# Moving the first score products of group 0 in layer 1 further back in TensorE's stream

## The chip, the cores and the metric

One core of a Trainium2 chip runs the whole computation in one launch. The metric is device time in microseconds (us); the kernel before took 1233.0 us, the median of three runs (1233.14, 1230.1 and 1233.0).

## The reference, cut to what matters

Two layers act on x (512 positions by 1024 features, fp32). Layer 0 has a mixer of gated linear attention and differential attention, layer 1 a mixer of dilated window attention; each is followed by a gated feed-forward block with a short convolution. The change lies in layer 1's mixer:

```
z = (h @ w_in).reshape(B, S, 3 groups, 3 (q, k, v), 4 heads, 128)
q = rmsnorm(z[:, :, :, 0], q_gain);  k = rmsnorm(z[:, :, :, 1], k_gain);  v = z[:, :, :, 2]
for each group g, (window, dilation) in (128, 1), (512, 4), (2048, 16):
    s = q k^T / sqrt(128), causal, inside the window, keys at stride dilation
    o_g = softmax(s) v,  lse_g = log of the softmax denominator
o = sum over g of softmax over g (lse_g) * o_g;   x = x + o @ w_out
```

## The kernel before, in words

**Products.** Every weight product is done in three passes: weights and activations are split into a high and a low part (`hi`, `lo`; `hhi`, `hlo`), and high times high, high times low and low times high are summed in PSUM. The weights come as a chain of slabs; `load_next` (L168 on) loads a slab through SP's queue, ScalarE makes `hi` (L179), VectorE makes `lo` (L182). There are three buffers for each, and a slab is asked for when the slab two places ahead of it is begun.

**Layer 1's mixer.** Its order is q, k of group 0, q, k of group 1, q, k of group 2, then v of the three groups. In this text they are q0, k0, q1, k1, q2, k2, v0, v1, v2. Each is a `tok_gemm` (L333): 4 slabs of 2 contraction chunks; for each slab the four position tiles t = 0 to 3 in turn, 6 products of 128x512 for a tile, so 24 a slab and 96 a projection. Each tile has a PSUM bank from a pool of eight (`bufs=8`). In the last slab a tile is complete after its 6 products and is evicted.

**Eviction of q and k** (`qk_evict`, L396 on): ScalarE squares the bank (L367), VectorE sums (L369), both work out the reciprocal root (L213 to L218), VectorE scales the bank into `qn` (L401, the last reader of the bank), VectorE turns 32x32 blocks (L387), ScalarE's queue writes them to DRAM (`turned`, L389), POOL's queue reads them back in four DMAs into `z` (L394; three `z` buffers), and ScalarE copies `z` into q (L416) or k (L414).

**Scores** (`scores`, L893 on). Group 0 has four steps, one for a query tile; each writes two banks (L901), 8 products of 128x128 in the first step and of 128x256 in the other three. All four k tiles of group 0 are needed for its first step, because its positions are stored by residue. Groups 1 and 2 use one bank a step (L912) and need only tile t of q and k. Behind each step VectorE masks and takes the row minimum (L282), ScalarE exponentiates (L891). After group 0's last step `residues` issues five small DMAs on POOL's queue (L930, L932), read much later in `factors`.

**What sets the order.** TensorE's order is written out by hand: `now` is a planned clock. Every step of a projection adds its planned time (`pe`), then `fire` runs each event that is due. In `tok_gemm` a step is one tile of one slab: 6 products, 3 * 2 * 512 * 0.216 / 512 = 1.296 us of planned time. An event is put down with `at(delay, ...)`. The copy of tile t into q or k is due 11.5 + t after its eviction; behind the copy of k's last tile `after_k` puts down the first score step; each score step adds its own planned time (0.86 or 1.73 us in group 0) and puts down the next 5.0 later. The orders of the other engines are worked out from the program when it is built.

Of the kernel before, what the change touches and what calls it, by code (L numbers as in the profile page):

```python
# [129 lines left out]
def trunk_kernel(ctx: ExitStack, tc: tile.TileContext, x, weights, params, lqks, w_a2, consts, out):  # L130
# [12 lines left out]
    def bank():  # L143
        return ps.tile([P, 512], F32, name="bank")
# [147 lines left out]
    def at(delay, fn, tag):  # L292
        count[0] += 1
        heapq.heappush(events, (now[0] + delay, count[0], tag, fn))
# [5 lines left out]
    def pe(us):  # L300
        now[0] += us
# [132 lines left out]
    with tc.tile_pool(name="m0", bufs=1) as m0, tc.tile_pool(name="t0", bufs=2) as t0:  # L434
        def t8(name, dt=F32):
            return m0.tile([P, 4, 512], dt, name=name, tag="t8", bufs=8)
# [143 lines left out]
        def after_k(t):  # L580
            if t == NT - 1:
                at(1.0, lambda: diff_scores(0), "diff")
# [288 lines left out]
    with tc.tile_pool(name="m1", bufs=1) as m1:  # L871
# [13 lines left out]
        def probs(dst, sc, g, t, h):  # L885

            nk = sc.shape[1]
            m = masks[:, 3 - nk // P:3].rearrange("p a b -> p (a b)") if g == 0 else masks[:, 3 * (g - 1)]
            nm = st[g][:, t, 0, h:h + 1]
            masked(dst, sc, m, nm)  # L890
            A.activation(dst, dst, AF.Exp, bias=nm, scale=-1.0, accum_out=st[g][:, t, 1, h:h + 1])  # L891

        def scores(g, t, q, k):  # L893
            ts = slice(t * P, (t + 1) * P)
            if g == 0:
                nk = P if t == 0 else 2 * P
                for hp in range(2):
                    sc = bank()
                    for h in range(2):
                        o = h * 256  # L900
                        T.matmul(sc[:, o:o + nk], q[:, 2 * hp + h, ts], k[:, 2 * hp + h, (t + 1) * P - nk:(t + 1) * P],  # L901
                                 start=(h == 0), stop=(h == 1))
                    pe(8 * nk * PASS)
                    for h in range(2):
                        b0 = max(0, 2 * t - 1)
                        dst = PR[0][:, 2 * hp + h, b0:b0 + nk // P].rearrange("p b k -> p (b k)")
                        probs(dst, sc[:, h * 256:h * 256 + nk], 0, t, 2 * hp + h)
            else:
                sc = bank()
                for h in range(4):  # L910
                    hs = slice(h * P, (h + 1) * P)
                    T.matmul(sc[:, hs], q[:, h, ts], k[:, h, ts], start=(h == 0), stop=(h == 3))  # L912
                pe(0.87)
                for h in range(4):
                    probs(PR[g][:, h, t], sc[:, h * P:(h + 1) * P], g, t, h)
            if t < NT - 1:
                at(5.0, lambda: scores(g, t + 1, q, k), "scores")
            elif g == 0:
                residues()
            elif g == 2:  # L920
                factors()
# [6 lines left out]
        def residues():  # L928

            G.dma_start(d0, st0.rearrange("p t a h -> p t (a h)"))  # L930
            for t in range(NT):
                G.dma_start(s0[32 * t:32 * t + 32].rearrange("p r a h -> p r (a h)"),  # L932
                            d0.rearrange("(r l) t c -> t l r c", r=4)[t])

        def factors():

            sn = [s0, st[1], st[2]]
            mx = m1.tile([P, NT, 4], F32, name="mx")
            V.tensor_tensor(out=mx, in0=sn[0][:, :, 0], in1=sn[1][:, :, 0], op=ALU.min)
            V.tensor_tensor(out=mx, in0=mx, in1=sn[2][:, :, 0], op=ALU.min)  # L940
            eg = m1.tile([P, 3, NT, 4], F32, name="eg")
            for g in range(3):
                V.tensor_tensor(out=eg[:, g], in0=mx, in1=sn[g][:, :, 0], op=ALU.subtract)
            A.activation(eg.rearrange("p g t h -> p (g t h)"), eg.rearrange("p g t h -> p (g t h)"), AF.Exp)
            den = m1.tile([P, NT, 4], F32, name="den")
            dt = m1.tile([P, NT, 4], F32, name="dt")
            V.tensor_tensor(out=den, in0=eg[:, 0], in1=sn[0][:, :, 1], op=ALU.mult)
            for g in (1, 2):
                V.tensor_tensor(out=dt, in0=eg[:, g], in1=sn[g][:, :, 1], op=ALU.mult)
                V.tensor_tensor(out=den, in0=den, in1=dt, op=ALU.add)  # L950
            V.reciprocal(den, den)
            for g in range(3):
                V.tensor_tensor(out=eg[:, g], in0=eg[:, g], in1=den, op=ALU.mult)

            G.dma_start(e0, eg[:, 0])
            for r in range(4):
                G.dma_start(f0[32 * r:32 * r + 32], e0.rearrange("(t l) r h -> r l t h", t=NT)[r])
            fac.extend((f0, eg[:, 1], eg[:, 2]))
            for i in range(12):
                at(10.0 + 3.5 * i, lambda i=i: weigh(i // 4, i % 4), "weigh")  # L960
# [32 lines left out]
        def after_k(g, q, k):  # L993
            def f(t):
                if t == NT - 1:
                    at(2.5 if g == 0 else 1.0, lambda: scores(g, 0, q, k), "scores")
            return f

        def by_tile(dst, r):
# [9 lines left out]
        for g in range(3):  # L1009
            q, k = t8("q"), t8("k")  # L1010
# [41 lines left out]
```

## Time and profile before

| What | Value |
|---|---|
| Median of the runs | 1233.0 us (1230.1 to 1233.14, 3 runs) |
| Profiled execution, own time | 1230.4 us |
| Profiled execution, span | 1228.6 us |
| Mean granted TensorE clock | 0.997 of full speed |
| DMA over the span | mean 103 GB/s |

The profile lists one execution. PE is TensorE's products, PEld its weight loads, DVE VectorE, ACT ScalarE, POOL GpSimd. A busy time counts instructions that do work; a wait is put down to the instruction that came last. Starts are us from the start of the span, durations in us.

### The profile page before, as it was taken

What the parts mean: (1) busy time and instruction counts of PE and PEld (TensorE: products, weight loads), DVE (VectorE), ACT (ScalarE), POOL (GpSimd) and SP (SyncE); (2) the same over time, 40 slices, a digit from 0 to 9 for tenths busy, and PEclk for the clock granted to TensorE, in tenths of its full rate; (3) what the DMA queues carried; (4) which work ended last, traced back from release to release, by engine and by line L of the source; (5) the groups of instructions that cost most, each with busy time, mean ns of one, the idle gap of its engine ahead of it and who ended that gap; (6) DMA issues with size and microseconds to landing.
All of it is one profiled execution on the core that took longest, in us unless ns stands there. A gap on an engine that the chain in (4) does not pass through costs nothing.

```text
span 1228.6 us, 15071 instructions
## 1 busy us (share of the span) xinstructions
PE 1215.2 (99%) x5687; PEld 1006.4 (82%) x5687; DVE 779.3 (63%) x1474; ACT 546.6 (44%) x896; POOL 68.4 (6%) x131
## 2 busy tenths in 40 slices
PE   9999999999999999999998999999999999999998
PEld 7888788788888888888886888889888888888887
DVE  7557868787753775366756676444877537763673
ACT  6446655454422443144534655544544314431441
POOL 0000000000000000000022324300000000000000
PEclk9999999999999999999999999999999999999999
DMA  7222111323323323332455456421233232332322
GB/s 256 87 87 70 49 56 38 100 88 102 103 86 103 99 91 103 94 91 71 137 159 169 123 162 203 140 87 51 88 103 95 94 103 93 96 103 88 101 77 95
DMA packets 41160, 127.14 MB, mean 103 GB/s; under 512 B 6359, under 2 KB 7288, under 8 KB 41088
## 3 DMA queue, kind: packets, MB, share of 16 engines
q1 hardware_dynamic: 32400, 110.38, 29.1%
q0 software_dynamic: 3936, 7.41, 2.3%
q10 hardware_dynamic: 4752, 8.39, 1.8%
q8 instruction: 44, 0.72, 0.2%
q14 instruction: 28, 0.23, 0.1%
HBM read 116.70 MB, written 8.41 MB: 102 GB/s over the span
## 4 chain that ended last, share of the span: by engine, by line
PE 95%; DMA 2%; DVE 1%; POOL 1%; ACT 0%; issue 0%; SPq 0%; POOLq 0%; ACTq 0%; DVEq 0%
PE bank L766 39%; PE bank L333 22%; PE bank L808 20%; PE bank L350 7%; DMA z<-turned 1%; PE bank L989 1%; PE bank L536 1%; PE bank L570 1%; DMA turned<-turn 1%; PE bank L901 1%; PE bank L912 1%; PE bank L379 1%; POOL z L394 1%; PE bank L974 1%; PE bank L558 0%; PE bank L664 0%
## 5 line engine op out<-in xcount | busy, mean ns | idle before, releaser
L179 ACT ACTIVATE hi<-raw 128x1024 fp32r<-128x1024 f32 (+2 forms) x209 | 217.0, 1039 | 280.7 <-PE bank L808 143.2
L182 DVE TENSOR_TENSOR lo<-raw,hi 128x1024 fp32r<-128x1024 f32 (+2 forms) x209 | 250.5, 1199 | 128.8 <-ACT hi L179 120.1
L766 PE MATMUL bank<-hhi,hi 128*128 128x512 f32 x704 | 273.9, 389 | 0.0
L766 PE MATMUL bank<-hhi,lo 128*128 128x512 f32 x704 | 273.9, 389 | 0.0
L766 PE MATMUL bank<-hlo,hi 128*128 128x512 f32 x704 | 273.9, 389 | 0.0
L333 PE MATMUL bank<-hi,hhi 128*128 128x512 f32 (+2 forms) x480 | 185.2, 386 | 0.5 <-ACT hi L179 0.5
L333 PE MATMUL bank<-lo,hhi 128*128 128x512 f32 (+2 forms) x480 | 181.1, 377 | 0.2 <-DVE lo L182 0.2
L333 PE MATMUL bank<-hi,hlo 128*128 128x512 f32 (+2 forms) x480 | 180.5, 376 | 0.0
L766 PEld LDWEIGHTS bank<-hhi,hi 128*128 128x128 f32 x704 | 132.2, 188 | 27.5
L766 PEld LDWEIGHTS bank<-hhi,lo 128*128 128x128 f32 x704 | 132.2, 188 | 27.4
L766 PEld LDWEIGHTS bank<-hlo,hi 128*128 128x128 f32 x704 | 132.2, 188 | 27.3
L808 PE MATMUL bank<-ghi,lo 128*128 128x512 f32 (+1 forms) x358 | 138.0, 385 | 0.0
L808 PE MATMUL bank<-glo,hi 128*128 128x512 f32 (+1 forms) x358 | 138.0, 385 | 0.0
L808 PE MATMUL bank<-ghi,hi 128*128 128x512 f32 (+1 forms) x358 | 138.0, 385 | 0.0
L333 PEld LDWEIGHTS bank<-lo,hhi 128*128 128x128 f32 x480 | 90.4, 188 | 17.7 <-DVE lo L182 1.0
L333 PEld LDWEIGHTS bank<-hi,hhi 128*128 128x128 f32 x480 | 90.6, 189 | 17.1 <-ACT hi L179 1.0
L333 PEld LDWEIGHTS bank<-hi,hlo 128*128 128x128 f32 x480 | 90.7, 189 | 15.4
L813 DVE TENSOR_TENSOR xT<-xT,bank 128x512 f32<-128x512 f32 (+1 forms) x49 | 33.0, 675 | 106.4 <-PE bank L808 106.2
L394 POOL DMA_DIRECT2D z<-turned x96 | 52.0, 549 | 514.0 <-DVE rs_a L213 435.9
L808 PEld LDWEIGHTS bank<-ghi,hi 128*128 128x128 f32 x358 | 67.2, 188 | 13.6
L808 PEld LDWEIGHTS bank<-glo,hi 128*128 128x128 f32 x358 | 67.2, 188 | 13.5
L808 PEld LDWEIGHTS bank<-ghi,lo 128*128 128x128 f32 x358 | 67.3, 188 | 13.5
(203 smaller groups left out, 1358.7 us busy)
## 6 DMA issues: line engine op xcount, KB each, us to landing
raw<-in_weights_dram SPq DMA_DIRECT2D x189, 512.0 KB, 3.5
raw<-in_weights_dram SPq DMA_DIRECT2D x16, 384.0 KB, 3.1
turned<-turn ACTq DMA_DIRECT2D x24, 256.0 KB, 2.9
z<-turned POOLq DMA_DIRECT2D x96, 64.0 KB, 3.8
xT<-in_xT_dram SPq DMA_DIRECT2D x7, 256.0 KB, 5.8
out_dram<-xT ACTq DMA_DIRECT2D x7, 256.0 KB, 2.0
raw<-in_weights_dram SPq DMA_DIRECT2D x2, 544.0 KB, 3.5
vt<-vs POOLq DMA_DIRECT2D x16, 64.0 KB, 2.2
```

The lines of the kernel that those rows point to most:

```text
L179: r = A.activation(hi[:, c0:c1], raw[:, c0:c1], AF.Copy)
L182: V.tensor_tensor(out=lo[:, c0:c1], in0=raw[:, c0:c1], in1=hi.bitcast(F32)[:, c0:c1], op=ALU.subtract)
L333: T.matmul(ps[t][:, :n], lhs(a[:, kc], t), b[:, k, :n], start=(kc == 0 and j == 0), stop=(kc == DC - 1 and j == 2))
L350: T.matmul(ps, w[:, k, d * P:(d + 1) * P], r(k), start=(k == 0 and j == 0), stop=(k == nk - 1 and j == 2))
L379: T.transpose(pt[:, h * P:(h + 1) * P], src[:, h * P:(h + 1) * P], ident)
L394: G.dma_start(to[32 * j:32 * j + 32].rearrange("c i b r -> c i (b r)"), d[j])
L536: T.matmul(sc[:, :nk], qT[rs, h, n * P:(n + 1) * P], kT[rs, h, :nk], start=True, stop=True)
L570: T.matmul(po[n][:, h * P:(h + 1) * P], wT[:, j * P:(j + 1) * P], bv[:, j, h * P:(h + 1) * P], start=(h == 0 and j == 0), stop=(h == 3 and ...
L766: T.matmul(ps, w[:, kc], r[:, kc], start=(kc == 0 and m == 0), stop=(kc == DC - 1 and m == 2))
L808: T.matmul(ps[:, ts], a[:, k], b[f0 + k][:, ts], start=(k == 0 and m == 0), stop=(k == n - 1 and m == 2))
L813: V.tensor_tensor(out=xT[:, c, ts], in0=xT[:, c, ts], in1=ps[:, ts], op=ALU.add)
L901: T.matmul(sc[:, o:o + nk], q[:, 2 * hp + h, ts], k[:, 2 * hp + h, (t + 1) * P - nk:(t + 1) * P], start=(h == 0), stop=(h == 1))
```

## The change

The delay between the last k copy and the first score step of group 0 goes from 2.5 to 10.5 on the planned clock. Nothing else is edited.

```
         def after_k(g, q, k):
             def f(t):
                 if t == NT - 1:
-                    at(2.5 if g == 0 else 1.0, lambda: scores(g, 0, q, k), "scores")
+                    at(10.5 if g == 0 else 1.0, lambda: scores(g, 0, q, k), "scores")
             return f
```

## Rows read from the trace of the kernel before

**Rows 1.** The page: part 1 (busy time, share of the span, instructions of each engine) and the first line of part 4 (share of the chain that ended last, by engine).
```profile
PE 1215.2 (99%) x5687; PEld 1006.4 (82%) x5687; DVE 779.3 (63%) x1474; ACT 546.6 (44%) x896; POOL 68.4 (6%) x131
PE 95%; DMA 2%; DVE 1%; POOL 1%; ACT 0%; issue 0%; SPq 0%; POOLq 0%; ACTq 0%; DVEq 0%
```

**Rows 2.** The view of waits of the whole span: engine, tile and line, what it waited for, us in total, times, longest.
```profile
PEld bank L901 <- ACT k L414: 6.2, 1, 6.2
PE bank L901 <- ACT k L414: 5.8, 1, 5.8
...
PEld bank L570 <- issue: 2.9, 5, 0.8
```

**Rows 3.** The timeline of PE around group 0's first score step: start, duration, instruction; in brackets the idle time before it and its releaser.
```profile
649.70 0.39 PE L333 MATMUL bank<-hi,hhi 128*128 128x512 f32 x1
...
667.15 0.39 PE L333 MATMUL bank<-lo,hhi 128*128 128x512 f32 x1
673.35 2.08 PE L901 MATMUL bank<-k,q 128*128 128x128 f32 x8 [5.81 <-ACT k L414]
675.08 0.77 PE L333 MATMUL bank<-hi,hhi 128*128 128x512 f32 x1
675.65 0.63 PE L333 MATMUL bank<-hi,hlo 128*128 128x512 f32 x1
...
681.54 1.89 PE L901 MATMUL bank<-k,q 128*128 128x256 f32 x8
```

**Rows 4.** Windows: length, busy time and count of each engine, granted clock, share of the DMA engines, GB/s.
```profile
649.60:667.40 17.80, 17.80 (x80) 14.52 (x78) 10.78 (x33) 5.67 (x13) 7.26 (x14) 1.00 0.57 169
667.40:673.40 6.00, 0.19 (x2) 0.05 (x1) 5.04 (x10) 3.28 (x7) 1.42 (x3) 0.73 0.67 209
673.40:677.20 3.80, 3.80 (x14) 3.37 (x15) 1.03 (x9) 1.73 (x8) 1.17 (x3) 0.53 0.24 88
677.20:707.30 30.10, 30.10 (x135) 25.15 (x134) 18.98 (x61) 18.73 (x49) 10.23 (x19) 1.00 0.46 133
```

**Rows 5.** The chain that ended last, in order of time: start, length, what, with the number of products.
```profile
673.35 2.08 PE bank L901 x8
675.43 6.27 PE bank L333 x24
681.70 1.73 PE bank L901 x8
683.42 5.45 PE bank L333 x24
...
697.78 25.85 PE bank L333 x114
723.64 0.89 PE bank L912 x8
724.53 5.46 PE bank L333 x24
729.98 0.89 PE bank L912 x8
```

**Rows 6.** Timelines of ACT and POOL: the way of k0's last tile (k0's first copy, which frees the buffer; the four reads into z; the square of q1's tile 0; k0's last copy).
```profile
665.50 0.63 ACT L414 ACTIVATE k<-z 128x512 f32<-128x512 f32 x1 [8.25 <-DMA turned<-turn]
...
666.65 2.17 POOL L394 DMA_DIRECT2D z<-turned  x4 [0.42 <-issue]
...
668.98 0.67 ACT L367 ACTIVATE sq<-bank,rstd 128x512 f32<-128x512 f32 x1
...
672.67 0.63 ACT L414 ACTIVATE k<-z 128x512 f32<-128x512 f32 x1 [1.58 <-DMA z<-turned]
```

**Rows 7.** The timeline of DVE: the scaling of a bank into qn, after which the bank is free. In order: k0's tiles 0, 1 and 3; q1's tiles 0, 1 with 2, and 3; k1's tile 1.
```profile
651.08 0.69 DVE L401 TENSOR_TENSOR qn<-bank,rr 128x512 f32<-128x512 f32 x1
...
654.29 0.68 DVE L401 TENSOR_TENSOR qn<-bank,rr 128x512 f32<-128x512 f32 x1
...
659.60 0.68 DVE L401 TENSOR_TENSOR qn<-bank,rr 128x512 f32<-128x512 f32 x1
...
671.97 0.69 DVE L401 TENSOR_TENSOR qn<-bank,rr 128x512 f32<-128x512 f32 x1
...
684.09 1.28 DVE L401 TENSOR_TENSOR qn<-bank,rr 128x512 f32<-128x512 f32 x2
...
687.99 0.69 DVE L401 TENSOR_TENSOR qn<-bank,rr 128x512 f32<-128x512 f32 x1
...
710.96 0.68 DVE L401 TENSOR_TENSOR qn<-bank,rr 128x512 f32<-128x512 f32 x1
```

**Rows 8.** Timelines of ACT and DVE: the two parts of k1's second slab (hi on ACT, lo on DVE).
```profile
667.51 1.04 ACT L179 ACTIVATE hi<-raw 128x1024 fp32r<-128x1024 f32 x1
...
668.58 1.23 DVE L182 TENSOR_TENSOR lo<-raw,hi 128x1024 fp32r<-128x1024 f32 x1 [0.24 <-ACT hi L179]
```

**Rows 9.** Timelines of POOL and ACT: the five DMAs of `residues`, the first reads of k1's tiles, and the copy of k1's tile 0.
```profile
700.07 0.57 POOL L930 DMA_DIRECT2D d<-st  x1 [4.92 <-ACT PR L891]
702.07 2.17 POOL L932 DMA_DIRECT2D s<-d  x4 [1.44 <-DMA d<-st]
711.90 2.17 POOL L394 DMA_DIRECT2D z<-turned  x4 [7.66 <-DMA turned<-turn]
...
716.44 0.63 ACT L414 ACTIVATE k<-z 128x512 f32<-128x512 f32 x1 [2.51 <-DMA turned<-turn]
```

More of the change, by code (lines that the diff above doesn't have):

```diff
@@ L995, in f @@
                 if t == NT - 1:
-                    at(2.5 if g == 0 else 1.0, lambda: scores(g, 0, q, k), "scores")
+                    at(10.5 if g == 0 else 1.0, lambda: scores(g, 0, q, k), "scores")
             return f
```

## The prediction

> **What bounds the kernel now.** I began with the page's shares: TensorE is busy for 1215.2 of 1228.6 us and holds 95% of the chain that ended last [rows 1]. So only two things can change the time: the work TensorE does, which the edit leaves as it is, and the 13.4 us in which it stands still. The view of waits says where these are. One wait stands out: group 0's first score step waits once, for 5.8 us (6.2 on the weight loads), for ScalarE's copy into k; the next largest entry of TensorE in the answer is 2.9 us in five pieces [rows 2]. Then I read TensorE's timeline there. The 78 products of q1 from 649.70 to 667.15 run evenly, (667.15 - 649.70) / 77 = 0.2266 us apart. The next would have started at 667.38; instead the score products start at 673.35 [rows 3]. The granted clock says what else the pause costs: 1.00 before it, 0.73 in it and 0.53 in the 3.8 us behind it, so most of that stretch ran at the lower level, 1.2 instead of 2.4 GHz [rows 4].
>
> **What the change removes.** (a) The wait: 673.35 - 667.38 = 5.97 us [rows 3]. (b) The slow stretch: from the start of the first score step to that of the second are 681.54 - 673.35 = 8.19 us [rows 3]. Group 1's first step is also 8 products of 128x128 with 24 projection products behind it, and takes 0.89 + 5.46 = 6.35 at the full clock [rows 5]. The excess is 1.84 us. Together 7.81 us, if the step finds everything ready at its new place.
>
> **Where it is put.** A step on the planned clock is 1.296 us and six products. A delay of 2.5 needs two steps, one of 10.5 nine (10.5 / 1.296 = 8.1). So the first score step moves back by seven steps, 42 products: the 18 that q1 has left after 78, and 24, all of k1's first slab. At 0.2266 us, q1 then ends at 667.38 + 4.08 = 671.46 and TensorE arrives at the score step at 667.38 + 9.52 = 676.90. The spacing to the next steps stays at 24 products, as the chain shows now [rows 5], so the four steps stand behind k1's product 24, 48, 72 and 96.
>
> **Is the operand there?** k0's last tile has its reads issued at 666.65 and its copy at 672.67, done at 673.30 [rows 6]. All that leads to it (the buffer freed by the copy at 665.50, the reads) lies before 667.38, the first moment at which the two streams differ. So 3.60 us are in hand. What could take them is ScalarE's order: with TensorE running on, the squares of q1's tiles 1 to 3 become ready between 669 and 672. In the trace the square of tile 0 (668.98) already stands ahead of that copy, and ScalarE then waits 1.58 us for the transfer [rows 6]. Bounds: nothing (squares fill that idle time), or, if the copy stood behind all of q1's eviction, as late as that ends now after q1's end, see below. I take nothing.
>
> **Are the weights there?** k1's second slab has both parts done at 668.58 + 1.23 = 669.81 [rows 8]; its products come behind the moved step, after 677. Cost nothing; the cover is 7 us.
>
> **Are the banks there?** This is what is late next. At its old place the step runs while q1 holds four of the pool's eight banks and k0's four are free. At its new place k1 holds those four, so the step needs two of q1's, and tile 0's and tile 1's must have been scaled out. Tile 0's is: 671.97 + 0.69 = 672.66 [rows 7], against 676.90. Tile 1's is needed half a step later, at 676.90 + 0.45 = 677.35, which is 5.89 us after q1's end. How long after its projection's end a tile 1 was done, from the rows: k0 654.29 + 0.68 - 649.70 = 5.3; k1, which ended at 697.78 + 42 x 0.2266 = 707.30, 710.96 + 0.68 - 707.30 = 4.3; q1 now, where a score step falls amid its eviction, ended at 681.54 - 6 x 0.2266 = 680.2 and needed until 684.09 + 0.64 = 684.7, so 4.5 [rows 3, 5, 7]. All three are below 5.89, by 0.6 to 1.6 us. A last tile took up to 659.60 + 0.68 - 649.70 = 10.6 [rows 7]; as an upper bound for tile 1 that is a wait of 4.7 us, and up to 1.84 for the clock. I take nothing, by the nearest rows, tile 1's own. The second step needs tiles 2 and 3 by 684.1, 12.6 after q1's end, over 10.6. The fourth step now falls at k1's end, so that q2's third and fourth tile need banks of k1 4.4 and 5.8 us after that end; k1's tile 0 serves the third, its tile 1 at 4.3 to 5.3 the fourth.
>
> The Trainium skill has a rule against this change: in PSUM — Partial Sum Buffer, "Summary: rules for kernel authors", it says "Evacuate promptly — 2 MiB is tight". By it the eight banks would decide, and the sum would be that of the first rival below. The trace agrees as far as the margin is thin, 0.6 us at least; it has no run with the step at that place.
>
> **What moves along.** The copies and exponentials of the four steps are the same instructions, on engines that were busy for 18.98 (VectorE) and 18.73 (ScalarE) of 30.1 us [rows 4], and keep their cover. `residues` moves too: its five DMAs on POOL's queue, at 700.07 to 704.24 now, before k1's first reads at 711.90 [rows 9]. In the new stream the fourth step ends 699.3 and k1 ends 697.6, so they meet k1's reads, wanted at 697.6 + (711.90 - 707.30) = 702.2. The residues' own reader, `factors`, comes after group 2's last step, so they may wait. If instead they go first, POOL waits in order: now the first is issued 700.07 - 697.78 = 2.3 us after the last score product, the next four 2.0 later, for 2.17 [rows 5, 9]. From 699.3 that ends at 705.8 and holds k1's reads by 3.6 us. Group 1's first step also moves: it is due one step after the copy of k1's last tile, 14.5 planned us after an eviction that comes one step before k1's end. Now that is 11 + 1 steps, q2's product 72 (114 = 42 + 72 in the chain [rows 5]); with the fourth group-0 step's 1.73 inside it, (14.5 - 1.3 - 1.73) / 1.296 gives 9 + 1, product 60. That is 712.9 in time; its k tile is copied at 697.6 + (716.44 + 0.63 - 707.30) = 707.4, 5.5 us in hand, over 3.6. Cost nothing; at the other end (the exponentials as late as q1's last tile now, 687.99 + 0.69 - 680.2 = 8.5 [rows 7], for 2.3) 9.8 - 5.5 = 4.3 us and up to 1.84 for the clock. From group 2's first step (v0's product 72) the stream is as before.
>
> **The sum.** 1230.4 (the profiled execution's own time, 1228.6 span) - 7.8 = 1222.6. The median of the runs is 2.6 above that execution; against the median it is 1233.0 - 7.8 = 1225.2, which I give. A measurement tells from no change about 0.3%, 3.7 us, so this is twice that.
>
> **The rivals.** *One wait comes back at the new place* (tile 1's bank, or k0's copy behind q1's evictions). For it: 0.6 us of margin on the bank, and two engines whose order is worked out anew. Against it: three tile-1 rows below the limit, and a copy with 3.6 in hand. Up to 4.7 + 1.84 = 6.5 us are given back: 1225.2 to 1231.8. *Residues ahead of k1's reads*: up to 4.3 + 1.84 = 6.1 given back, so 1225.2 to 1231.3; against it, k1's reads are asked for first in the program. *Slower*: the banks run out twice. Place: both banks of the first step and then of the second, with q1's eviction as late as k0's last tile or later; price 6.5 each, 13.0 against 7.8, so 1238.3. It decides from the point where tile 1's bank is free 7.8 us after it is needed, at 685.2 or 13.7 after q1's end; the latest eviction in these rows is 10.6. *Nothing shown*: the wait goes and an order elsewhere, worked out anew, costs the same: 1232.
>
> **How the numbers follow.** Forecast 0.70, at 1222.3 (from the lowest run, 1230.1) to 1226.5. One wait back 0.15, of which 0.06 stays better than 3.7 us. Residues 0.05 and nothing shown 0.03, both within 0.3%. Slower 0.07. Faster 0.76, same 0.09 + 0.05 + 0.03 = 0.17, slower 0.07. The range takes the forecast and two thirds of the one wait, 0.80: 1221.5 to 1230.5.
>
> **What would show it.** Right: the entry of L901 on the k copy gone from the waits; group 0's four steps behind k1's products 24, 48, 72 and 96; the clock 1.00 all through; group 1's first step behind q2's product 60; no idle time on TensorE from q1 to q2. Wrong: idle time before the second half of the first score step, released by VectorE's qn; a k copy that starts after 676.3; a gap at q2's third or fourth tile; a granted clock below 1 in k1; k1's reads on POOL behind the residues and L912 waiting for k.

## The result and the profile after

| | before | after |
|---|---|---|
| median (lowest to highest), us | 1231.9 (1230.1 to 1233.14), 6 runs | 1224.45 (1223.76 to 1227.03), 6 runs |
| ratio after / before | | 0.9946, interval 0.9936 to 0.9956 |
| profiled execution, us | 1230.4 | 1223.76 |
| span, us | 1228.6 | 1222.0 |
| granted clock, mean | 0.997 | 1.000 |

The change takes 7.45 us off the median; by the interval, 5.4 to 7.9 us (0.0044 and 0.0064 of 1231.9). 7.8 was forecast. A second comparison of the same two kernels (change_again, below) gave 4.38 us. An execution starts a little earlier or later, so for the accounts below I use a **stage**: in the chain that ended last, from the second sum of squares ahead of layer 1's projections (L252) to the first L974. Before, that is 804.33 - 616.37 = 187.96 us, after 797.68 - 616.86 = 180.82, so -7.14. From group 2's first score step to the end the two are alike: 1228.6 - 770.78 = 457.82 and 1222.0 - 764.13 = 457.87.

The first part of the page of after, beside [rows 1]:
```profile
PE 1214.3 (99%) x5687; PEld 1006.0 (82%) x5687; DVE 778.2 (64%) x1474; ACT 544.9 (45%) x896; POOL 68.5 (6%) x131
```
The same instructions, with TensorE standing still for 7.7 us (1222.0 - 1214.3) where it was 13.4. The waits of after (engine, tile, line, what for, us in total, times, longest), beside [rows 2]:
```profile
PEld bank L570 <- issue: 2.9, 5, 0.8
...
PEld bank L901 <- DVE qn L401: 0.6, 1, 0.6
...
PE bank L901 <- DVE qn L401: 0.4, 1, 0.4
```
The wait for k is gone and a small one for a bank stands in its place. Where it is shows in the timeline of PE (start, duration, instruction, idle time before it), beside [rows 3]:
```profile
677.16 0.39 PE L333 MATMUL bank<-lo,hhi 128*128 128x512 f32 x1
677.39 0.60 PE L901 MATMUL bank<-k,q 128*128 128x128 f32 x4
678.39 0.71 PE L901 MATMUL bank<-k,q 128*128 128x128 f32 x4 [0.39 <-DVE qn L401]
...
684.41 1.89 PE L901 MATMUL bank<-k,q 128*128 128x256 f32 x8
```
The first half of the step runs at once, the second waits for the scaling of a tile of q1. Half a step is 0.45 us, so the second half was due at 677.84 and is 0.55 late. From the first step's start to the second's are 7.02 us, 0.67 over the 6.35 of an undisturbed one [rows 5]. And 7.81 - 0.67 = 7.14, the whole change of the stage.

Windows of after (length, busy time and count of each engine, granted clock, DMA share, GB/s), beside [rows 4]:
```profile
667.40:677.20 9.80, 9.80 (x45) 8.10 (x44) 8.28 (x20) 6.94 (x16) 1.82 (x4) 1.00 0.56 168
677.20:700.00 22.80, 22.41 (x104) 18.77 (x103) 14.06 (x48) 14.34 (x41) 8.68 (x16) 1.00 0.62 173
```
The clock is 1.00 where it was 0.73 and 0.53. The chain that ended last, after, beside [rows 5]:
```profile
672.66 0.63 ACT k L414
673.29 0.09 ACT rs_y L214
...
675.59 1.12 DVE lo L182
...
677.74 0.60 DVE qn L401
678.34 0.04 issue
678.39 0.71 PE bank L901 x4
679.10 5.47 PE bank L333 x24
684.57 1.73 PE bank L901 x8
...
700.65 13.61 PE bank L333 x60
714.27 0.89 PE bank L912 x8
```
The spacing is 24 products, and group 1's first step stands behind q2's product 60. What I had not foreseen is where the chain shown here begins: it is still ScalarE's copy into k. What follows it is no longer the score step but, behind it in ScalarE's order, a root (L214) for q1's tile 1, from which VectorE's scaling and so the bank follow. The timelines of ACT and of DVE, beside [rows 6, 7]: the k copy and the root, then the operand of that root and the scalings of q1's tiles 0 and 1:
```profile
672.66 0.63 ACT L414 ACTIVATE k<-z 128x512 f32<-128x512 f32 x1 [1.19 <-DMA z<-turned]
673.20 0.19 ACT L214 ACTIVATE rs_y<-rs_a 128x4 f32<-128x4 f32 x1
```
```profile
671.61 0.17 DVE L213 TENSOR_SCALAR rs_a<-ss 128x4 f32<-128x4 f32 x1
...
672.36 0.69 DVE L401 TENSOR_TENSOR qn<-bank,rr 128x512 f32<-128x512 f32 x1
...
677.65 0.68 DVE L401 TENSOR_TENSOR qn<-bank,rr 128x512 f32<-128x512 f32 x1
```
The root's operand was done at 671.78, but the root starts at 673.20, as the copy ends. Tile 0 was scaled before the copy, tile 1 4.99 us after the copy's start: 1.43 us until ScalarE has made the root (copy, L214, L215; VectorE takes it up at 674.09), then 3.56 in which VectorE also does the sums of tiles 2 and 3, tile 0's turn and a part of the weights (L182, 1.12 in the chain). POOL's queue, beside [rows 9]:
```profile
717.44 2.17 POOL L394 DMA_DIRECT2D z<-turned  x4 [5.05 <-DMA turned<-turn]
719.60 0.56 POOL L930 DMA_DIRECT2D d<-st  x1
721.73 2.17 POOL L932 DMA_DIRECT2D s<-d  x4 [1.57 <-DMA d<-st]
```
The five DMAs of `residues` went behind k1's last reads, as forecast.

### The profile page after: what moved, and what is told of

The parts are those of the page before. It is cut to its first block, busy times and chain, and to the rows that moved or that the text cites. A ratio compares the mean times of both kernels' runs of the same rounds, so it can differ in the third digit from the quotient of the medians.

```text
span 1222.0 us, 15071 instructions
## 1 busy us (share of the span) xinstructions
PE 1214.3 (99%) x5687; PEld 1006.0 (82%) x5687; DVE 778.2 (64%) x1474; ACT 544.9 (45%) x896; POOL 68.5 (6%) x131
## 4 chain that ended last, share of the span: by engine, by line
PE 94%; DMA 2%; DVE 2%; ACT 1%; issue 0%; POOL 0%; SPq 0%; POOLq 0%; DVEq 0%
PE bank L766 39%; PE bank L333 21%; PE bank L808 20%; PE bank L350 7%; PE bank L989 1%; DMA z<-turned 1%; PE bank L536 1%; DMA turned<-turn 1%; PE bank L570 1%; PE bank L912 1%; PE bank L379 1%; PE bank L974 1%; PE bank L901 0%; DVE lo L182 0%; POOL z L394 0%
## 5 line engine op out<-in xcount | busy, mean ns | idle before, releaser
L179 ACT ACTIVATE hi<-raw 128x1024 fp32r<-128x1024 f32 (+2 forms) x209 | 217.0, 1039 | 277.8 <-PE bank L808 143.2
L182 DVE TENSOR_TENSOR lo<-raw,hi 128x1024 fp32r<-128x1024 f32 (+2 forms) x209 | 250.5, 1199 | 129.9 <-ACT hi L179 120.9
```

Of the source, the lines that this page charges most:

```text
L179: r = A.activation(hi[:, c0:c1], raw[:, c0:c1], AF.Copy)
L182: V.tensor_tensor(out=lo[:, c0:c1], in0=raw[:, c0:c1], in1=hi.bitcast(F32)[:, c0:c1], op=ALU.subtract)
```

## The experiments

Each ran beside the kernel before on the same chip. The last three columns are of one profiled execution, all in us: "stage", its change against 187.96; "k copy", when the copy of k0's last tile starts, counted from the stage's start, and in brackets how long the third copy into q0, some 29 us before it on ScalarE, waited for its transfer (kernel before: 56.30 (0.48); change: 55.80 (0.39)); "idle", the waits of TensorE over 0.3 that bear on it ("k", for a k copy; "bank", for a scaling into qn; "other", for another instruction).

| kernel | median (runs) | before (runs) | ratio, interval | stage | k copy | idle |
|---|---|---|---|---|---|---|
| scores_read_q | 1226.64 (5) | 1232.51 (17) | 0.9953, 0.9941 to 0.9966 | -3.98 | 57.64 (2.04) | bank 3.56 |
| delay_5_1 | 1230.78 (12) | 1232.51 | 0.9976, 0.9965 to 0.9987 | -3.57 | 55.57 (0.38) | k 2.37 |
| delay_7_7 | 1226.85 (5) | 1232.51 | 0.9957, 0.9945 to 0.9970 | -4.93 | 56.81 (0.63) | k 0.88, bank 1.12 |
| delay_12_9 | 1224.82 (5) | 1232.51 | 0.9938, 0.9926 to 0.9950 | -6.27 | 55.64 (0.51) | bank 1.27 |
| fill_26 | 1230.07 (11) | 1231.77 (24) | 0.9984, 0.9976 to 0.9993 | -1.41 | 56.59 (0.75) | none |
| delay_0_0 | 1234.60 (12) | 1231.77 | 1.0020, 1.0011 to 1.0029 | +2.32 | 55.32 (0.53) | k 7.55 |
| delay_9_0 | 1226.65 (5) | 1231.77 | 0.9956, 0.9943 to 0.9968 | -3.17 | 57.24 (2.18) | bank 2.50 |
| group1_at_72 | 1228.28 (7) | 1231.77 | 0.9967, 0.9955 to 0.9979 | -3.68 | 56.43 (2.06) | bank 1.01, 0.96, 1.35 |
| one_bank_10_5 | 1225.74 (6) | 1230.90 (13) | 0.9955, 0.9943 to 0.9967 | -4.51 | 57.32 (1.77) | other 0.77, k of group 1 0.35, other 1.64 |
| one_bank_9_0 | 1226.86 (8) | 1230.90 | 0.9972, 0.9960 to 0.9983 | -0.59 | 58.01 (2.56) | k 0.72, other 2.06, bank 0.86 |
| change_again | 1226.52 (5) | 1230.90 | 0.9965, 0.9953 to 0.9977 | -3.70 | 57.61 (2.06) | bank 2.19 |
| copy_behind_tile_1 | 1227.31 (5) | 1232.16 (9) | 0.9956, 0.9942 to 0.9969 | -3.50 | 62.54 (2.67) | k 2.52 |

The brackets fall into two kinds, 0.4 to 0.8 and 1.8 to 2.7, though all kernels are alike up to there; change_again, below, follows the cause. 187.96 is of the first kind, so I set a stage of the second against another of the second. No traced execution of the kernel before is of the second kind; its wait for k would be longer there by what its copy is later, so the gain from like to like in that kind may be larger than the table's (not shown). The bracket does not fix the copy's time by itself: delay_7_7, of the first kind, has it at 56.81, and group1_at_72, of the second, at 56.43.

**The wait alone: scores_read_q.** The step stays at its old place, but its operand is there early: group 0 scores q against q, so group 0's attention weights are others.
```diff
-  at(2.5 if g == 0 else 1.0, lambda: scores(g, 0, q, k), "scores")
+  at(2.5 if g == 0 else 1.0, lambda: scores(g, 0, q, q if g == 0 else k), "scores")
```


> Kernel before, delay 2.5, group 0's scores taken as q times q, so that the k copies are made but no score product reads them (the attention weights of group 0 are then others). My theory (the lost time is the wait for the last k copy, 5.97 us, and the slow clock behind it, 1.84): both go with the place of the step unchanged; 1231.9 - 7.8 = 1224.1, up to 1224.7 if k1's fourth tile waits for q1's tile 1 to be scaled out. No entry of L901 on a k copy, granted clock 1.00. Rival (the gain comes from the new place itself: other order on VectorE and ScalarE, group 1's steps 12 products earlier): stays at 1231.9 less at most 1 us.

The waits hold no L901 on k. But the timeline of PE has a new one:
```profile
682.25 0.47 PE L333 MATMUL bank<-hi,hhi 128*128 128x512 f32 x1 [3.56 <-DVE qn L401]
```
k1's fourth tile finds no bank until q1's tile 1 has been scaled. Of the 7.81 us the trace keeps 3.98 and the runs 5.87 (1232.51 - 1226.64), where I had expected nearly all. The changed kernel in an execution of the same kind keeps 3.70 (change_again): with the transfers that late, either place runs into q1's eviction, and the step's own operand is no longer what decides.

**How far back: delay_5_1, delay_7_7, delay_12_9.** The steps go back by 12, 24 and 48 products in place of 42.
```diff
-  at(2.5 if g == 0 else 1.0, lambda: scores(g, 0, q, k), "scores")
+  at(5.1 if g == 0 else 1.0, lambda: scores(g, 0, q, k), "scores")    # or 7.7, or 12.9
```


> Delay 5.1: four planned steps, 12 products behind the old place. TensorE arrives at 670.1 on the trace of before and waits about 3.2 us for the k copy, whose time does not move. Theory: 1231.9 - 7.8 + 3.2 = 1227.3 if the shorter pause leaves the clock at its upper level, 1229.1 if the granted clock falls as it did behind the long one (6.35 or 8.19 us from the first score step to the second). Rival (a fixed cost for any wait there): 1231.

> Delay 7.7: six planned steps, 24 products behind the old place, after k1's tile 0. Theory with banks: TensorE arrives about 0.5 us before the k copy is done, then takes k0's last free banks for the score step, and k1's tile 2 has to wait for q1's tile 1 to be scaled out (done about 6.4 us after q1's end, needed about 4.1 after it): 0.5 + 2.3 of the 7.8 stay, 1226.9, with a wait of a projection product (L333) on qn L401. Rival (the k copy is the only thing that counts, banks were a one-off of 0.6 us): 1224.6 and no wait but 0.5 us on k.

> Delay 12.9: ten planned steps, 48 products behind the old place, k1's product 30. Theory with banks: the second bank is wanted 1.4 us later than in the changed kernel, which waited 0.55 for it: that wait is gone and the whole 7.8 shows, 1224.1 (0.5 below the changed kernel, read from the trace more than from the times). The last score step then falls inside q2 and meets k1's eviction; a wait of up to 2 us on a bank there would give 1226. Rival (later is always worse, since k1's own eviction is what is hit): 1226 to 1228.

The timelines of PE, of delay_5_1, delay_7_7 and delay_12_9 in turn:
```profile
674.62 1.67 PE L901 MATMUL bank<-k,q 128*128 128x128 f32 x8 [2.37 <-ACT k L414]
```
```profile
673.99 1.16 PE L901 MATMUL bank<-k,q 128*128 128x128 f32 x8 [0.88 <-ACT k L414]
...
679.04 0.50 PE L333 MATMUL bank<-hi,hhi 128*128 128x512 f32 x1 [1.12 <-DVE qn L401]
```
```profile
705.54 0.47 PE L333 MATMUL bank<-hi,hhi 128*128 128x512 f32 x1 [1.27 <-DVE qn L401]
```
The wait for k shrinks as the step goes back, 5.81, 2.37, 0.88 and none, and the medians fall in that order. In delay_5_1's trace the pause is 3.44 shorter than before, but from the first step to the second are still 682.68 - 674.62 = 8.06 us, 1.71 over 6.35, with a granted clock of 0.79: the shorter pause cost nearly the whole 1.84 of the longer one, and 3.44 + 0.13 is the stage's -3.57. Its median, 1230.78, lies above both values of the theory, at the rival's 1231; seven of its twelve runs, 1230.69 to 1231.57, are slower than the traced one (1228.82), and no trace shows why. delay_7_7's median is where it was expected, its waits are not: k 0.88 for 0.5, and 1.12 for 2.3 on a bank, at k1's last tile. Once k is there a wait for a bank takes over, at a place that depends on where the step stands. delay_12_9's interval overlaps with the changed kernel's first one (0.9936 to 0.9956) and lies below its second (0.9953 to 0.9977), so 10.5 is not shown to be the best place, and 12.9 not shown to be a better one.

**Earlier still: delay_0_0.** Twelve products forward, with only the length of the wait in play.
```diff
-  at(2.5 if g == 0 else 1.0, lambda: scores(g, 0, q, k), "scores")
+  at(0.0 if g == 0 else 1.0, lambda: scores(g, 0, q, k), "scores")
```


> Delay 0: the first score step two planned steps, 12 products, ahead of its old place. Theory: the k copy's time does not depend on the place, so TensorE waits 12 x 0.2266 = 2.7 us longer, about 8.6, and the time is 1231.9 + 2.7 = 1234.6; the stretch behind it stays at 8.2 us. Rival (the copy also comes earlier or later with the place): 1231 to 1232, or over 1236.

The timeline of PE:
```profile
673.30 2.07 PE L901 MATMUL bank<-k,q 128*128 128x128 f32 x8 [7.55 <-ACT k L414]
...
682.07 1.89 PE L901 MATMUL bank<-k,q 128*128 128x256 f32 x8
```
1234.6 against 1231.77, +2.8, where 12 x 0.2266 = 2.7 more of waiting says +2.7. In the trace the wait is 7.55 - 5.81 = 1.74 longer, with a copy that came 1.0 sooner (55.32 for 56.30), and the stretch behind it is 8.77 where 8.19 was expected to stay; 1.74 + 0.58 is the stage's +2.32. A place ahead of the copy costs the products that could have stood there.

**The clock alone: fill_26.** The wait is filled with 26 products that nobody reads, so that TensorE does not pause.
```diff
+  def fill():
+      b = bank()
+      for _ in range(26):
+          T.matmul(b, hhi[:, DC - 1, :P], hhi[:, DC - 1], start=True, stop=True)
-  at(2.5 if g == 0 else 1.0, lambda: scores(g, 0, q, k), "scores")
+  at(2.5 if g == 0 else 1.0, lambda: (fill() if g == 0 else None, scores(g, 0, q, k)), "scores")
```


> Kernel before, delay 2.5, with 26 products of 128x512 into a bank that nobody reads put just ahead of the first score step: 26 x 0.2266 = 5.9 us of work in the place of the 5.97 us wait. Theory (1.84 of the 7.8 us is the clock that falls in the pause): the granted clock stays 1.00, first to second score step 6.35 us and not 8.19; 1231.9 - 1.8 = 1230.1. Rival (the slow stretch behind the pause has another cause, such as late operands of the score step): 8.19 stays, 1231.9.

The timeline of PE:
```profile
669.69 6.05 PE L996 MATMUL bank<-hhi 128*128 128x512 f32 x26
675.95 1.16 PE L901 MATMUL bank<-k,q 128*128 128x128 f32 x8 [0.20 <-ACT k L414]
...
682.43 1.89 PE L901 MATMUL bank<-k,q 128*128 128x256 f32 x8
```
From the first step to the second are 6.48 us in place of 8.19 [rows 3]: 1.71 of the forecast's 1.84. The step starts 675.95 - 669.69 = 6.26 after the moment at which it could have, 0.29 more than before (the copy came later), and 1.71 - 0.29 = 1.42 is the stage's -1.41. In the runs it is 1.7 us (by the interval 0.9 to 3.0). The window from the first step to the second (length, busy time and count of each engine, granted clock, DMA share, GB/s):
```profile
675.95:682.43 6.48, 6.48 (x32) 5.51 (x33) 3.92 (x18) 4.60 (x15) 1.48 (x3) 1.00 0.19 71
```
The clock is 1.00 where it was 0.53 behind the pause. The clock's part of the sum is shown.

**Another place for the bank wait: delay_9_0.** Thirty products back.
```diff
-  at(2.5 if g == 0 else 1.0, lambda: scores(g, 0, q, k), "scores")
+  at(9.0 if g == 0 else 1.0, lambda: scores(g, 0, q, k), "scores")
```


> Delay 9.0: seven planned steps, 30 products behind the old place, behind k1's tile 1. Theory with banks: no wait for the k copy (arrival 674.2 against 673.3), the score step takes the last two free banks, and k1's tile 3 waits about 1.4 us for q1's tile 1: 1225.5, a wait of L333 on qn L401 and none of L901. Rival (only the k copy): 1224.1 and no wait.

```profile
680.02 0.50 PE L333 MATMUL bank<-hi,hhi 128*128 128x512 f32 x1 [2.50 <-DVE qn L401]
```
In this line of PE's timeline the wait is where it was expected, for the tile that was expected, but 2.50 long; the granted clock behind it is 0.80 (676 to 684). The size is taken up under change_again.

**Group 1 kept at q2's product 72: group1_at_72.** My forecast had put this shift at nothing.
```diff
-  at(10.5 if g == 0 else 1.0, lambda: scores(g, 0, q, k), "scores")
+  at((10.5, 3.6, 1.0)[g], lambda: scores(g, 0, q, k), "scores")
```


> Changed kernel (delay 10.5 for group 0), with group 1's delay 3.6 in place of 1.0, so that its first score step stands behind q2's product 72 again, as before the change. Theory: that shift is free, same time as the changed kernel, 1224.5, the trace without a wait at L912. Rival (part of the gain comes from group 1's steps standing earlier): 1226 to 1228.

```profile
680.63 0.71 PE L901 MATMUL bank<-k,q 128*128 128x128 f32 x4 [1.01 <-DVE qn L401]
...
731.53 0.47 PE L333 MATMUL bank<-hi,hhi 128*128 128x512 f32 x1 [0.96 <-DVE qn L401]
...
734.51 1.13 PE L912 MATMUL bank<-k,q 128*128 128x128 f32 x8 [1.35 <-DVE qn L401]
```
The lines are of PE's timeline. The second and third, 2.3 us, are in neither trace of the changed kernel: at 72 group 1's steps meet q2's eviction. The theory that the shift does nothing falls in the trace. The stage gives 7.81 - 3.68 = 4.13 less than forecast; the first step loses 686.65 - 679.01 - 6.35 = 1.29 of it, and the 2.84 left are for the most part these two waits. That change_again's stage, -3.70, is as long does not make the shift free: there the first step alone loses 4.10, behind a copy that came 1.18 later. So a part of what the changed kernel keeps depends on group 1's steps standing at 60, as the rival has it. In the times it is not shown: 0.9967 stands beside 0.9946 and 0.9965.

**Fewer banks for the step: one_bank_10_5, one_bank_9_0.** The first step's four heads of 128 columns share one bank.
```diff
-  for hp in range(2):
+  n = 4 if t == 0 else 2
+  for hp in range(4 // n):
...
-      for h in range(2):
-          o = h * 256
-          T.matmul(sc[:, o:o + nk], q[:, 2 * hp + h, ts], ..., start=(h == 0), stop=(h == 1))
+      for h in range(n):
+          o = h * (512 // n)
+          T.matmul(sc[:, o:o + nk], q[:, n * hp + h, ts], ..., start=(h == 0), stop=(h == n - 1))
...
-  at(2.5 if g == 0 else 1.0, lambda: scores(g, 0, q, k), "scores")
+  at(10.5 if g == 0 else 1.0, lambda: scores(g, 0, q, k), "scores")    # or 9.0
```


> Changed kernel (delay 10.5), but the first score step puts its four heads' 128 columns each into one PSUM bank and not two; the other three steps as before; nothing is left out. Theory (what is left of the 7.8 us is the wait for q1's tile 1 to be scaled out, because k1 and q1 hold all eight banks): the step needs q1's tile 0 alone, done 4 us earlier; no wait of L901's kind on qn L401, and from the second rstd product of layer 1 to the first transposition of the weights 7.7 to 7.8 us less than before (the changed kernel: 7.14). In the times 0.6 us, too little to see: 1224. Rival (the wait is VectorE's order, not the number of banks): 0.5 to 1 us of waiting stays.

> Delay 9.0 with the first score step in one bank. With two banks this place lost 2.5 us to k1's fourth tile waiting for q1's tile 1, and the granted clock fell to 0.80 behind it. Theory: with one bank less in use the fourth tile gets q1's tile 0's; wait and slow clock are gone, 7.3 to 7.8 us less than before where two banks gave 3.2; 1224.3. At most 0.5 us of waiting for the k copy. Rival (the place itself is bad, whatever the banks): 3 to 4 us less, 1227.5.

In both the bank wait that the edit aimed at is gone. PE's timelines, of one_bank_10_5 and then of one_bank_9_0, have others further on:
```profile
703.90 0.47 PE L333 MATMUL bank<-hi,hhi 128*128 128x512 f32 x1 [0.77 <-ACT rs_y L215]
...
800.73 1.50 PE L976 MATMUL bank<-cst,PR 128*128 128x128 f32 x7 [1.64 <-DVE PR L969]
```
```profile
730.54 0.47 PE L333 MATMUL bank<-hi,hhi 128*128 128x512 f32 x1 [2.06 <-DVE rs_u L216]
```
The banks were the cause of the wait in the first step: in one_bank_10_5 it takes 684.15 - 677.81 = 6.34 to the second, undisturbed. Taking it away earned nothing that the times show, and one_bank_9_0's median, 1226.86, is near its rival's 1227.5; its profiled execution, the slowest, keeps 0.59 of the stage. That the order of VectorE and ScalarE further on came out another way is where the new waits point; it was not tested. Neither version is shown to beat the changed kernel.

**The same kernel once more: change_again.** The changed kernel unedited, beside the two above.

> The changed kernel once more, unedited, beside the two others on the same chip: what one profile's waits differ by from another's. 1224.5 (0.9946 of before); the wait of L901 on qn L401 between 0.3 and 1.2 us.

The ratio is 0.9965, 4.38 us (1230.90 - 1226.52; by the interval 2.8 to 5.8) where the first comparison gave 7.45, and the profiled execution, 1229.04 us, is the slowest of this kernel's. Its timeline of PE, and the windows around it:
```profile
679.25 0.60 PE L901 MATMUL bank<-k,q 128*128 128x128 f32 x4
682.05 1.22 PE L901 MATMUL bank<-k,q 128*128 128x128 f32 x4 [2.19 <-DVE qn L401]
...
689.70 1.89 PE L901 MATMUL bank<-k,q 128*128 128x256 f32 x8
```
```profile
676.00:684.00 8.00, 5.80 (x27) 4.84 (x26) 6.48 (x22) 4.51 (x11) 2.17 (x4) 0.88 0.44 153
684.00:692.00 8.00, 8.00 (x34) 6.63 (x33) 4.96 (x15) 3.82 (x11) 5.12 (x10) 0.91 0.80 233
```
From step to step are 10.45 us, 4.10 over 6.35, and the stage gives 7.81 - 3.70 = 4.11 less than forecast: this wait (682.05 against 679.70, so 2.35) and the clock behind it (1.75) are all of it. Then its timelines of ACT and DVE, with the third copy into q0, the k copy and tile 1's scaling:
```profile
647.90 0.72 ACT L416 ACTIVATE q<-z,prm 128x512 f32<-128x512 f32 x1 [2.06 <-DMA z<-turned]
...
676.33 0.63 ACT L414 ACTIVATE k<-z 128x512 f32<-128x512 f32 x1 [1.66 <-DMA z<-turned]
```
```profile
681.31 0.69 DVE L401 TENSOR_TENSOR qn<-bank,rr 128x512 f32<-128x512 f32 x1
```
Tile 1 again follows the k copy by 4.98 us. So it does in group1_at_72 (674.91 to 679.89), delay_7_7 (673.31 to 678.29), delay_9_0 (674.30 to 679.29), delay_12_9 (672.69 to 677.67) and both one_bank kernels: 4.98 or 4.99 each time. Where the first score step stands ahead of q1's end it is otherwise, from 3.67 (delay_5_1) to 13.70 (delay_0_0). Counted from the stage's start, the copy came at 55.80 in the first profile of the changed kernel, at 57.61 here and at 57.24 in delay_9_0: 1.81 later here, and the bank wait is 2.19 - 0.39 = 1.80 longer. In group1_at_72 (56.43) the copy is 0.63 later and the wait 1.01 - 0.39 = 0.62 longer. delay_9_0's surplus is of the same kind.

Why was the copy late? In the first profile the same q0 copy had hardly waited for its transfer (its timeline of ACT):
```profile
644.40 0.72 ACT L416 ACTIVATE q<-z,prm 128x512 f32<-128x512 f32 x1 [0.39 <-DMA z<-turned]
```
It starts 29.18 us into the stage here and 27.54 there. Behind it on ScalarE stand a part of the weights (L179) and the squares of k0's tile 0, whose scaling then comes 35.69 instead of 34.33 into the stage, the reads of k0's last tile 51.47 instead of 50.19, and the k copy last. The instructions of the two executions are the same, so the spread of this kernel's runs (11 in two comparisons, 1223.76 to 1229.04, median 1226.48) can come from one transfer that lands some 2 us sooner or later. Of the 14 profiled executions, seven have the short wait and seven the long one; the timed runs without a profile show no such column, so their shares stay unknown.

**The link cut: copy_behind_tile_1.** In the changed kernel the k copy is put behind tile 1's squares and roots on ScalarE (`hold` is 3.8 for k0, else 0), TensorE's order being the same.
```diff
-  A.activation(to, pt, AF.Copy)
+  c = A.activation(to, pt, AF.Copy)
+  if hold and t == NT - 1:
+      tc.keep_in_program_order(c)
-  at((11.5 if turned is not None else 6.5) + t, tr, tag)
+  at((11.5 if turned is not None else 6.5) + t + (hold if t == NT - 1 else 0.0), tr, tag)
-  at(10.5 if g == 0 else 1.0, lambda: scores(g, 0, q, k), "scores")
+  at(6.6 if g == 0 else 1.0, lambda: scores(g, 0, q, k), "scores")    # counted from the copy, now due 3.8 later
```


> Changed kernel with TensorE's order unedited, but k0's last copy put behind q1's tile 1 on ScalarE's queue: its due time is three planned steps later (and the score step's delay three less), and it is pinned behind what ScalarE was given before it. In the two profiles of the changed kernel the scaling of q1's tile 1 starts 4.99 and 4.98 us after the start of that copy, whenever the copy's transfer lands. Theory (ScalarE takes its work in order, so that the late copy holds q1's tile 1 and with it the bank): now tile 1 is scaled before the copy starts, the wait of L901 on qn L401 is gone, and the score step waits for the copy instead, some 0.3 to 1.5 us, because the copy stands behind two DMA issues; 1224 to 1225.5. Rival (tile 1 is late by VectorE's own load): the scaling stays some 5 us behind the copy, or as late as before, and the wait on qn stays.

Its timelines of DVE, of ACT and of PE:
```profile
679.32 0.68 DVE L401 TENSOR_TENSOR qn<-bank,rr 128x512 f32<-128x512 f32 x1
```
```profile
681.31 0.63 ACT L414 ACTIVATE k<-z 128x512 f32<-128x512 f32 x1 [1.42 <-DVE rs_u L217]
```
```profile
681.99 2.08 PE L903 MATMUL bank<-k,q 128*128 128x128 f32 x8 [2.52 <-ACT k L414]
```
Tile 1 is scaled 60.55 us into the stage, where change_again, whose q0 copy had waited long as well, had it at 62.59: 2.0 sooner without the copy ahead of it. Of this 0.4 was there at tile 0 already (56.40 and 56.83), so some 1.6 are the copy's, and the link is shown, in one trace. VectorE's 3.54 us from tile 1's root (675.78) to its scaling are as long as before: that part of the 4.98 is not the copy's. The wait for the bank is gone. But the copy came at 681.31, behind the roots of tiles 2 and 3 as well, more than meant, and the score step waits 2.52 us for it, more than expected; so the time, 1227.31, is not the 1224 to 1225.5 of the theory, and the stage, -3.50, is no better than change_again's -3.70.

## Why the prediction was right, step by step

- **What is removed** came as worked out: the 5.97 us of waiting and the 1.84 of the lower clock. fill_26 takes the clock's part away alone (1.71), delay_0_0 and delay_5_1 change the wait for the most part (1.74 of 2.32, 3.44 of 3.57), and in both profiles of the changed kernel 7.81 less what the first step loses there (0.67; 4.10) is the stage's change (7.14; 3.70).
- **The number.** That the first comparison gave 7.45, so near to 7.8, is luck in part: the same two kernels gave 4.38 in the second, also inside the range, but with as much given back as the rival of one wait coming back allows for, and neither trace keeps the whole 7.81.
- **Operand.** Right: k is copied at 673.29, 4.1 us before the step arrives, and in change_again at 676.96, 2.3 before.
- **Weights, residues, the places of the steps.** Right: no wait for weights, `residues` behind k1's reads, steps 24 products apart, group 1 at 60 with its k copied at 712.06 for 714.27, 2.2 in hand where 5.5 were forecast.
- **"Are the banks there? I take nothing."** This term was mis-sized. It is 0.67 us in one profile and 4.10 in the other, clock included, within the 4.7 + 1.84 given as its upper bound. I had taken a tile 1's lateness from its projection's end, 4.3 to 5.3 against a limit of 5.89, and so a margin of 0.6. Counted so, q1's tile 1 was done 6.4 and 8.2 us after q1's end (671.95 and 673.81, 24 products ahead of the step). In this place it goes by the k copy: tile 1 is scaled 4.98 us after the copy begins, and its bank is free 5.7 after, because its root stands behind the copy in ScalarE's order and VectorE then needs 3.55 us, for the most part with work of other tiles; how much of that another order would spare is not shown. That ScalarE waits for the copy's transfer stood in [rows 6]; I asked whether the copy would be late for the score step, not who stands behind it. The Trainium skill's rule that was set against the change (PSUM — Partial Sum Buffer, "Summary: rules for kernel authors", to evacuate promptly) agrees with the trace in this much: 0.39 and 2.19 us of waiting for a bank, and 3.56 at the old place once the wait for k was taken away.
- **The rival** "one wait comes back at the new place" is what happens, at its small end in the first profile and past its middle in the other. The slower rival's banks running out twice did not occur.
- **"Cost nothing" for group 1's shift** holds in both traces of the changed kernel, with no wait at its steps. That the shift spares something, two bank waits of 2.3 us in the trace of group1_at_72, I had not seen.

What stays open: why the runs of one kernel lie up to 6 us apart, delay_5_1's above all (1225.6 to 1231.57), when at most two executions of a kernel have a trace; why the built order of VectorE and ScalarE gives bank waits from q2 to k2 in some of these kernels and none in the kernel before, and what makes the q0 transfer land early or late.

## What to carry to other kernels

A matmul that waits for another engine's copy can be put later by at least as many products as the wait is long (5.97 / 0.2266, some 26 here), and the loss by the clock goes with the wait; but then look at what else stands behind that copy on its own engine. Here ScalarE kept to its order, so the late copy held the root behind it (ready at 671.78, started at 673.20), and with it the eviction whose bank the moved step needed: the same transfer still set the time, though it cost less. Thirty products (delay_9_0) met another bank wait, 2.50 us, so the length of the wait alone does not give the place. Before a margin of half a microsecond is taken as enough, ask how much its ends move from one execution to another: here it was 1.8 us.

## What the runs showed of the hardware

The length of a pause alone does not set the clock behind it. In change_again TensorE had worked without a break in the 16 us up to 676, at a granted clock of 1.00. After 2.19 us of waiting the two windows from 676 to 692 have 0.88 and 0.91 on the mean; the projection products were 0.43 us apart up to 685.2, about twice the 0.2266 of the full clock, so this is the lower of its two levels, and then 0.23. In delay_5_1 a wait of 2.37 us cost 1.71 us behind it, nearly as much as the 1.84 behind the 5.81 of the kernel before. In scores_read_q a wait of 3.56 us left the clock at 1.00, the 2.4 GHz level, in the three windows from 668 to 692; the one with the wait in it:
```profile
676.00:684.00 8.00, 4.44 (x20) 3.36 (x19) 8.00 (x26) 3.99 (x12) 2.18 (x4) 1.00 0.40 124
```
What tells these pauses apart is not shown.
